# The first 128 queries' scores by products of 256 columns, the two halves added by VectorE

## The chip, the cores and the metric

The kernel runs on one core of a Trainium2 chip. The metric is the device time of one execution in microseconds; below 0.2% two times of this kernel count as the same. The operands and the output are float32.

## The reference, cut to what matters

One decoder layer over 512 tokens of width 1024: a gated linear recurrence (HGRN2) and a multi-head latent attention (MLA, 8 heads) side by side, then a gated merge, an output product and a norm. The change is in the scores of the attention:

```python
def attend_block(blk):                       # blocks of 128 queries
    qn = q_nope[block]; qp = q_pe[block]     # 128 and 64 numbers per head
    s = (einsum('bqhd,bkhd->bhqk', qn, k_nope)
         + einsum('bqhr,bkr->bhqk', qp, k_pe)) * scale
    s = where(q_pos[:, None] >= key_pos[None, :], s, -inf)
    p = softmax(s, axis=-1)
    return einsum('bqhk,bkhd->bqhd', p, v)
```

`k_pe` is one rotary key for all heads. For the first 128 queries only the first 128 keys count.

## The kernel before, in words

**Numbers.** TensorE multiplies float32 values as pairs: a high part (the value rounded to the `F32R` format) and a low part (the rest). `split` (L158) makes them: ScalarE casts the high part (L160), VectorE subtracts it to get the low part (L161). `mm3` (L88) is a product of two such pairs: high by high (L91), high by low (L92), low by high (L93), three matmuls into one PSUM bank. Each matmul loads its own stationary operand (a weight load, PEld in the profile) and streams a moving one, 512 columns in most of them.

**Scores.** `mla_scores` (L708) treats the 512 queries of a head in four blocks of 128. Block `i` needs `n = 128 (i + 1)` keys, so its matmuls have 128, 256, 384 and 512 columns. Each block has five: three of `mm3` on the parts of q and k without position, and two (L718) with the rotary query, whose high and low parts lie in the two halves of the partitions, against the rotary key's high part and low part (`kpe[0]`, `kpe[1]`). VectorE then adds the causal mask onto the last 128 columns in PSUM (L721), takes the row maximum (L722) and scales it (L723); ScalarE takes the exponential (L724); VectorE inverts its sum (L725); GpSimd multiplies by that (L726; VectorE in the last head). Then TensorE transposes the result (L742).

**Order.** Head 0's scores stand in a TensorE order written out by hand (`last_outputs`). Those of heads 1 to 7 are placed by a planner, which simulates every engine by costs of its own and issues what is ready first by program order; so TensorE's order between the scores and the neighbouring products (the gate of the head, the keys and queries of the next one, the output of the one before) is the planner's. All queues are served in order once laid out.

**Tiles.** A pool hands out tiles by tag; with one buffer for a tag, whatever first writes a new tile of that tag waits until all that used the old one has ended. `qn`, `kn` and `qp` were two tiles each, one for the high and one for the low part (tags `qn0`, `qn1` and so on), `kpe` too. The tags of `qn`, `kn` and `qp` in the pool `ma_pool` serve twice: for the heads, and long before (71 to 110 us) in `early_sums` (L801), which forms sums of blocks of the normed input while the recurrence runs. Its `keep` (L811) splits a sum and stores both parts to DRAM from SP's queue (L815). `keep` runs four times per call with the tags qn, kn, qp, qn, and `early_sums` is called twice.

**PSUM.** Three of the eight banks (`mm_ps`, `N_MM = 3`) hold projections, five (`ax_ps`) the rest.

Of the kernel before, what the change touches and what calls it, by code (L numbers as in the profile page):

```python
# [9 lines left out]
F32 = mybir.dt.float32  # L10
F32R = mybir.dt.float32r
# [3 lines left out]
ALU = mybir.AluOpType  # L15
# [3 lines left out]
P = 128  # L19
D = 1024  # L20
S = 512
# [17 lines left out]
def hybrid_layer(ctx: ExitStack, tc: tile.TileContext, a):  # L39
    nc = tc.nc  # L40
# [13 lines left out]
    def mm_tile():  # L54
        return mm.tile([P, 512], F32, tag="mm", name="mm_ps")

    def ax_tile():
        return ax.tile([P, 512], F32, tag="ax", name="ax_ps")
# [4 lines left out]
    class Pool:  # L63


        def __init__(self, name, side):
            self.cm = tc.tile_pool(name=name, bufs=1, side=side, reuse_waits="tile")
            self.p = self.cm.__enter__()
# [16 lines left out]
    cpool = Pool("cpool", "right")  # L85


    def mm3(ps, l, r, lsl, rsl, start, stop):  # L88

        (lh, ll), (rh, rl) = l, r  # L90
        nc.tensor.matmul(ps, lh[lsl], rh[rsl], start=start, stop=False)  # L91
        nc.tensor.matmul(ps, lh[lsl], rl[rsl], start=False, stop=False)  # L92
        nc.tensor.matmul(ps, ll[lsl], rh[rsl], start=False, stop=stop)  # L93
# [5 lines left out]
    def load_w(*pieces, to=None):  # L99

        raw = wraw.tile([P, WCH], F32, tag="raw", name="w_raw")
        hi, lo = to or [pool.tile([P, WCH], F32R, tag=tag, name=f"w_{tag}")[:] for pool, tag in ((whi, "hi"), (wlo, "lo"))]
        views, o = [], 0
        for src in pieces:
            n = int(np.prod(src.shape[1:]))
            if len(src.shape) == 4:
                _, k, h, c = src.shape
                dst = raw[:, o : o + n].rearrange("p (k h c) -> p k h c", k=k, h=h)
                for i in range(k):
                    nc.sync.dma_start(dst[:, i], src[:, i])  # L110
            else:
                last_dma[0] = nc.sync.dma_start(raw[:, o : o + n].rearrange("p (k c) -> p k c", k=src.shape[1]), src)
                if queued:
                    with tc.issue_after(last_dma[0].ins):
                        queued.pop(0)()
            views.append([t[:, o : o + n].rearrange("p (k c) -> p k c", k=src.shape[1]) for t in (hi, lo)])
            o += n
        last_hi[0] = nc.scalar.copy(hi[:, :o], raw[:, :o])  # L118
        last_lo[0] = nc.vector.tensor_tensor(lo[:, :o], raw[:, :o], hi[:, :o].bitcast(F32), op=ALU.subtract)  # L119
        return views[0] if len(views) == 1 else views  # L120
# [6 lines left out]
    def proj_ch(mat, c0, rhs, hook=None):  # L127

        ps = [mm_tile() for _ in range(2)]
        for kh, w in enumerate(load_cols(mat, c0)):  # L130
            for m in range(2):
                if hook and kh and m:
                    hook()
                for k in range(4):
                    kk = 4 * kh + k
                    mm3(ps[m][:], w, rhs, (slice(None), k, slice(m * P, m * P + P)),
                        (slice(None), kk), kk == 0, kk == KD - 1)
        return ps
# [19 lines left out]
    def split(hi, lo, src):  # L158

        nc.scalar.copy(hi, src)  # L160
        nc.vector.tensor_tensor(lo, src, hi.bitcast(F32), op=ALU.subtract)  # L161
# [5 lines left out]


    cT = [cpool.tile([P, 5, S], F32R, f"cT{i}") for i in range(2)]
    kpe = [cpool.tile([P, S], F32R, f"kpe{i}") for i in range(2)]  # L170
    cw = Pool("cwork", "right")
    ktab = cw.tile([P, NT, 2, NR], F32, "ktab")
    c_sb = cw.tile([P, NT, 704], F32, "c_sb")
# [182 lines left out]
    ps = ax_tile()  # L356
# [9 lines left out]
    mask_inf = const.tile([P, P], F32, name="mask_inf")  # L366
# [23 lines left out]
    for t in range(NT):  # L390
        ps = mm_tile()
        for k in range(KD):
            mm3(ps[:, 0:448], hT, c_second[k // 2], (slice(None), k, slice(t * P, t * P + P)), (slice(None), k % 2),
                k == 0, k == KD - 1)
        nc.scalar.copy(c_sb[:, t, 256:704], ps[:, 0:448])
# [18 lines left out]
    for j in range(5):  # L414
        ps = ax_tile()
# [5 lines left out]
    ps = ax_tile()  # L421
    for t in range(NT):
        nc.tensor.transpose(ps[:, t * P : t * P + P], kd[:, t].rearrange("p a r -> p (a r)"), ident[:])
    split(kpe[0][:], kpe[1][:], ps[:])
    cw.close()


# [1 line left out]
    ma_pool = Pool("mla_a", "right")  # L429
# [197 lines left out]
    def low(w, k0, nk):  # L627
        ps = mm_tile()
        for k in range(nk):
            mm3(ps[:], w, cT, (slice(None), k), (slice(None), k0 + k), k == 0, k == nk - 1)  # L630
        return ps
# [21 lines left out]

    def mla_rope_hi(qr, qx):

        qp, qh = [ma_pool.tile([P, S], F32R, f"qp{i}") for i in range(2)], ma_pool.tile([P, S], F32R, "qh")
        with tc.issue_after(last_act[0].ins):
            nc.scalar.copy(qh[:], qx[:])
            for i in range(2):
                own = slice(64 * i, 64 * i + 64)  # L660
                nc.scalar.copy(qp[i][own], qr[own])
        return qp, qh, qx
# [9 lines left out]
    def mla_rope(qr, qx):  # L672
        return mla_rope_lo(*mla_rope_hi(qr, qx))
# [12 lines left out]
    def mla_nope(h, pool):  # L686
        wq, wk = load_w(w_uq[:, :, h, 0:128], w_ukv[:, :, h, 0:128])
        res = []
        for w, k0, nk, nm in ((wq, 0, 3, "qn"), (wk, 3, 2, "kn")):
            ps = low(w, k0, nk)  # L690
            t = [pool.tile([P, S], F32R, f"{nm}{x}") for x in range(2)]
            split(t[0][:], t[1][:], ps[:])
            res.append(t)
        return res

    def mla_gate(h, hook=None):
# [11 lines left out]
    def mla_scores(h, pool, qn, kn, qp, final=False):  # L708

        pn = []  # L710
        for i in range(NT):
            n = (i + 1) * P
            bl = slice(i * P, n)
            sps = ax_tile()
            qh = qp[h % 2]
            mm3(sps[:, :n], qn, kn, (slice(None), bl), (slice(None), slice(0, n)), True, False)
            for x in range(2):
                nc.tensor.matmul(sps[:, :n], qh[:, bl], kpe[x][:, :n], start=False, stop=x == 1)  # L718
            sm = pool.tile([P, 4], F32, "sm", 4)
            p = pool.tile([P, n], F32, f"p{i}")  # L720
            nc.vector.tensor_tensor(sps[:, bl], sps[:, bl], mask_inf[:], op=ALU.add)  # L721
            nc.vector.tensor_reduce(sm[:, 0:1], sps[:, :n], axis=AX.X, op=ALU.max, negate=True)  # L722
            nc.vector.tensor_scalar(sm[:, 1:2], sm[:, 0:1], SCALE, None, op0=ALU.mult)  # L723
            last_act[0] = nc.scalar.activation(p[:, :n], sps[:, :n], AF.Exp, scale=SCALE, bias=sm[:, 1:2], accum_out=sm[:, 2:3])  # L724
            last_dve[0] = nc.vector.reciprocal(sm[:, 3:4], sm[:, 2:3])  # L725
            scaled_p = (nc.vector if final else nc.gpsimd).tensor_scalar(p[:, :n], p[:, :n], sm[:, 3:4], 0.5,  # L726
                                                                         op0=ALU.mult, op1=ALU.mult)
            if not final:
                last_pool[0] = scaled_p
            pn.append(p)  # L730
        return pn
# [28 lines left out]
    def minus(out, x, y):  # L760
        nc.vector.tensor_tensor(out, x, y, op=ALU.subtract)

    def minus_minus(out, x, y):

        nc.vector.scalar_tensor_tensor(out, x, -1.0, y, op0=ALU.mult, op1=ALU.subtract)
# [33 lines left out]
    h_dram = [[dram.tile([P, 4, 256], F32, name=f"h{n}{i}") for i in range(2)] for n in range(1, 5)]  # L799

    def early_sums(q):  # L801

        E = lambda tag: ma_pool.tile([P, 2, 256], F32, tag)[:]
        h11, h12, h21, h22 = zip(*[[b[:, q] for b in blocks(t)] for t in hT])

        def whole(tag, hl):
            out = E(tag)
            nc.vector.tensor_tensor(out, hl[0].bitcast(F32), hl[1].bitcast(F32), op=ALU.add)
            return out

        def keep(n, tag, src):  # L811
            hl = [ma_pool.tile([P, 2, 256], F32R, f"{tag}{i}") for i in range(2)]
            split(hl[0][:], hl[1][:], src)
            for i in range(2):
                nc.sync.dma_start(h_dram[n - 1][i][:, q], hl[i][:].bitcast(F32))  # L815

        e22, e21, e11, e12 = whole("qr", h22), whole("qs", h21), whole("qh", h11), whole("p3", h12)
        minus(e22, e22, e21)
        keep(1, "qn", e22)
        minus_minus(e22, e22, e11)  # L820
        keep(2, "kn", e22)
        minus(e21, e11, e21)
        keep(3, "qp", e21)
        minus_minus(e12, e12, e22)
        keep(4, "qn", e12)
# [115 lines left out]
    qp, nope, pn = early  # L941
    late = None
    turned_q = mla_turn(1)
    for h in range(H):
# [5 lines left out]
        if h % 2 and h + 1 < H:  # L950
            qp = mla_rope(*turned_q)
# [292 lines left out]
```

## Time and profile before

| | |
|---|---|
| median of 3 runs | 612.52 us (612.38 to 612.58) |
| the profiled execution | 612.32 us, of which 610.5 us lie between its first and its last instruction |
| TensorE (PE) busy | 600.0 us, 98% |
| VectorE (DVE) busy | 434.5 us, 71% |
| ScalarE (ACT) busy | 285.4 us, 47% |
| GpSimd (POOL) busy | 151.8 us, 25% |
| matmuls of the scores | start from 272.9 to 392.3 us |

Times in the rows are us from the first instruction. A row's duration of a matmul holds its way through the array, so durations of neighbours overlap; what a matmul costs TensorE is the distance to the next one's start. A few matmul records are missing.

### The profile page before, as it was taken

How to read it: one execution, taken by the hardware profiler on the slowest of the kernel's cores; microseconds unless marked ns; L12 is line 12 of the kernel's file. 1: busy time of each engine (PE TensorE's matmuls, PEld its weight loads, DVE VectorE, ACT ScalarE, POOL GpSimd, SP SyncE). 2: the span in 40 equal slices, each digit the busy share in tenths (PEclk: the TensorE clock that was granted, in tenths of full speed). 3: DMA queues.
4: the chain of work that ended last, by engine and by line, in shares of the span. 5: the costliest groups of instructions: out<-in, count | busy, mean ns of one | idle time of the engine just before them, and what ended most of it. 6: DMA issues, size and time to landing. Idle time of an engine off the chain costs nothing.

```text
span 610.5 us, 9790 instructions
## 1 busy us (share of the span) xinstructions
PE 600.0 (98%) x3686; PEld 526.6 (86%) x3686; DVE 434.5 (71%) x679; ACT 285.4 (47%) x531; POOL 151.8 (25%) x253
## 2 busy tenths in 40 slices
PE   8999999999999999999999999999999999999994
PEld 5998888888888888888888888899999999888884
DVE  7717988589874639958767766747757678567885
ACT  5555245323313242435646455438757853434352
POOL 4106322354360136414263620400000000000011
PEclk9999999999999999999999999999999999999998
DMA  7549479996979966673469574956665565695103
GB/s 266 165 138 337 160 216 377 295 233 145 251 161 269 235 177 143 140 156 96 59 177 157 143 149 120 246 214 213 191 189 179 186 196 169 198 365 176 42 27 139
DMA packets 74544, 114.38 MB, mean 187 GB/s; under 512 B 7512, under 2 KB 41726, under 8 KB 74496
## 3 DMA queue, kind: packets, MB, share of 16 engines
q1 hardware_dynamic: 65100, 89.69, 45.7%
q0 software_dynamic: 8336, 22.55, 20.2%
q10 hardware_dynamic: 1060, 1.51, 0.7%
q8 instruction: 29, 0.48, 0.3%
q14 instruction: 19, 0.16, 0.1%
HBM read 105.34 MB, written 39.85 MB: 238 GB/s over the span
## 4 chain that ended last, share of the span: by engine, by line
PE 89%; DVE 6%; ACT 2%; issue 1%; DMA 0%; POOL 0%; POOLq 0%; ACTq 0%; DVEq 0%
PE mm_ps L91 19%; PE mm_ps L92 19%; PE mm_ps L93 19%; PE ax_ps L883 16%; PE mm_ps L883 3%; PE ax_ps L718 2%; PE mm_ps L271 1%; PE ax_ps L742 1%; PE ax_ps L551 1%; DVE w_lo L119 1%; DVE ya L1115 1%; PE ax_ps L93 1%; PE ax_ps L92 1%; PE ax_ps L91 1%; PE ax_ps L553 1%
## 5 line engine op out<-in xcount | busy, mean ns | idle before, releaser
L119 DVE TENSOR_TENSOR w_lo<-w_raw,w_hi 128x1024 fp32r<-128x1024 f32 (+3 forms) x116 | 137.2, 1196 | 75.3 <-ACT w_hi L118 69.5
L118 ACT CAST w_hi<-w_raw 128x1024 fp32r<-128x1024 f32 (+3 forms) x116 | 114.9, 1006 | 133.8 <-PE mm_ps L92 64.7
L91 PE MATMUL mm_ps<-hT,w_hi 128*128 128x512 f32 x320 | 125.9, 394 | 0.0
L92 PE MATMUL mm_ps<-hT,w_hi 128*128 128x512 f32 x320 | 125.2, 391 | 0.0
L93 PE MATMUL mm_ps<-hT,w_lo 128*128 128x512 f32 x320 | 124.8, 391 | 0.0
L93 PEld LDWEIGHTS mm_ps<-hT,w_lo 128*128 128x128 f32 x320 | 60.1, 188 | 12.3
L91 PEld LDWEIGHTS mm_ps<-hT,w_hi 128*128 128x128 f32 x320 | 60.1, 188 | 12.1
L92 PEld LDWEIGHTS mm_ps<-hT,w_hi 128*128 128x128 f32 x320 | 60.1, 188 | 11.7
L883 PE MATMUL ax_ps<-s,w_hi 128*128 128x256 f32 x384 | 54.1, 283 | 0.0
L883 PEld LDWEIGHTS ax_ps<-s,w_hi 128*128 128x128 f32 x384 | 49.7, 192 | 0.1
L1132 POOL TENSOR_SCALAR ssum<-ssum 128x1 f32<-128x1 f32 x3 | 0.9, 312 | 188.5 <-ACT sq L1119 188.5
L93 PE MATMUL mm_ps<-w_hi,hT 128*128 128x512 f32 (+1 forms) x96 | 36.5, 382 | 0.0
L92 PE MATMUL mm_ps<-w_lo,hT 128*128 128x512 f32 (+1 forms) x96 | 36.5, 382 | 0.0
L91 PE MATMUL mm_ps<-w_hi,hT 128*128 128x512 f32 (+1 forms) x96 | 36.2, 386 | 0.0
L724 ACT ACTIVATE p<-ax_ps,sm 128x128 f32<-128x128 f32 (+3 forms) x32 | 16.9, 528 | 34.4 <-DVE sm L723 34.0
L726 POOL TENSOR_SCALAR p<-p,sm 128x128 f32<-128x128 f32 (+3 forms) x28 | 15.7, 562 | 66.1 <-DVE sm L723 40.2
L883 PE MATMUL ax_ps<-s,w_lo 128*128 128x256 f32 x192 | 31.3, 284 | 0.2 <-DVE w_lo L119 0.2
L883 PEld LDWEIGHTS ax_ps<-s,w_lo 128*128 128x128 f32 x192 | 26.6, 192 | 0.4 <-DVE w_lo L119 0.4
L461 DVE RECIPROCAL tf<-pr 128x512 f32<-128x512 f32 x8 | 26.8, 3348 | 0.1
L91 PE MATMUL mm_ps<-cT,w_hi 128*128 128x512 f32 x52 | 20.7, 398 | 0.0
L93 PEld LDWEIGHTS mm_ps<-w_hi,hT 128*128 128x128 f32 x96 | 18.0, 188 | 3.1
L91 PEld LDWEIGHTS mm_ps<-w_hi,hT 128*128 128x128 f32 x96 | 18.0, 188 | 2.9
(299 smaller groups left out, 1211.3 us busy)
## 6 DMA issues: line engine op xcount, KB each, us to landing
w_raw<-w_in SPq DMA_DIRECT2D x54, 512.0 KB, 6.4
g_t<-w_in SPq DMA_DIRECT2D x16, 512.0 KB, 8.8
w_raw<-g_t SPq DMA_DIRECT2D x16, 512.0 KB, 4.3
g_t<-w_in POOLq DMA_DIRECT2D x8, 512.0 KB, 9.8
pa_t<-w_proj_a SPq DMA_DIRECT2D x8, 512.0 KB, 12.7
g_t<-g_t POOLq DMA_DIRECT2D x8, 512.0 KB, 10.1
out_t<-w_out SPq DMA_DIRECT2D x8, 512.0 KB, 8.6
s<-h POOLq DMA_DIRECT2D x8, 512.0 KB, 11.3
```

The costliest lines, as they stand in the source:

```text
L91: nc.tensor.matmul(ps, lh[lsl], rh[rsl], start=start, stop=False)
L92: nc.tensor.matmul(ps, lh[lsl], rl[rsl], start=False, stop=False)
L93: nc.tensor.matmul(ps, ll[lsl], rh[rsl], start=False, stop=stop)
L118: last_hi[0] = nc.scalar.copy(hi[:, :o], raw[:, :o])
L119: last_lo[0] = nc.vector.tensor_tensor(lo[:, :o], raw[:, :o], hi[:, :o].bitcast(F32), op=ALU.subtract)
L271: nc.tensor.matmul(ps, hT[l][:, 4 * kh + k, t * P : t * P + P], c_hl[kh][r][:, k * 256 : k * 256 + 256], start=kh == 0 and kind == 0 and k ...
L461: nc.vector.reciprocal(rp[:], pr[:])
L551: nc.tensor.matmul(ops[:, sl], asb[:, sl], v_sb[i][:, (h % 4) * P : (h % 4) * P + P], start=True, stop=i == 0)
L718: nc.tensor.matmul(sps[:, :n], qh[:, bl], kpe[x][:, :n], start=False, stop=x == 1)
L724: last_act[0] = nc.scalar.activation(p[:, :n], sps[:, :n], AF.Exp, scale=SCALE, bias=sm[:, 1:2], accum_out=sm[:, 2:3])
L726: scaled_p = (nc.vector if final else nc.gpsimd).tensor_scalar(p[:, :n], p[:, :n], sm[:, 3:4], 0.5, op0=ALU.mult, op1=ALU.mult)
L883: nc.tensor.matmul(ps[:, o], w[k // 2][i][:, k % 2, cols], ap[j][:, k], start=not banks and c == 0 and n == 0, stop=n == 11, skip_group_ch ...
```

## The change

A class `Pair` makes one tile of 2 x 512 columns look like the list of two that it replaces; `kpe`, `qn`, `kn`, `qp` and the tiles of `keep` become such pairs, high and low part side by side. In block 0 of each head the matmul against the key's high part and the one against its low part become one of 256 columns whose moving operand is two runs of 128 (columns 0 to 127 of the high part, and of the low part). The bank then holds two halves of partial scores, and VectorE adds the second half and the mask into the tile `p0`, and that onto the first half.

```diff
-    kpe = [cpool.tile([P, S], F32R, f"kpe{i}") for i in range(2)]
+    kpe = Pair(cpool.tile([P, 2, S], F32R, "kpe")[:])
...
-        qp, qh = [ma_pool.tile([P, S], F32R, f"qp{i}") for i in range(2)], ma_pool.tile([P, S], F32R, "qh")
+        qp, qh = Pair(ma_pool.tile([P, 2, S], F32R, "qp")[:]), ma_pool.tile([P, S], F32R, "qh")
...
-            t = [pool.tile([P, S], F32R, f"{nm}{x}") for x in range(2)]
-            split(t[0][:], t[1][:], ps[:])
-            res.append(t)
+            res.append(Pair(pool.tile([P, 2, S], F32R, nm)[:]))
+            split(*res[-1], ps[:])
...
-            mm3(sps[:, :n], qn, kn, (slice(None), bl), (slice(None), slice(0, n)), True, False)
-            for x in range(2):
-                nc.tensor.matmul(sps[:, :n], qh[:, bl], kpe[x][:, :n], start=False, stop=x == 1)
+            if i == 0:
+                wide = sps[:, : 2 * P].rearrange("p (x k) -> p x k", x=2)
+                nc.tensor.matmul(wide, qn[0][:, bl], kn.both[:, :, bl], start=True, stop=False)
+                nc.tensor.matmul(sps[:, bl], qn[1][:, bl], kn[0][:, bl], start=False, stop=False)
+                nc.tensor.matmul(wide, qh[:, bl], kpe.both[:, :, bl], start=False, stop=True)
+            else:
+                mm3(sps[:, :n], qn, kn, (slice(None), bl), (slice(None), slice(0, n)), True, False)
+                for x in range(2):
+                    nc.tensor.matmul(sps[:, :n], qh[:, bl], kpe[x][:, :n], start=False, stop=x == 1)
...
-            nc.vector.tensor_tensor(sps[:, bl], sps[:, bl], mask_inf[:], op=ALU.add)
+            if i == 0:
+                nc.vector.tensor_tensor(p[:], sps[:, P : 2 * P], mask_inf[:], op=ALU.add)
+            nc.vector.tensor_tensor(sps[:, bl], sps[:, bl], mask_inf[:] if i else p[:], op=ALU.add)
...
-            hl = [ma_pool.tile([P, 2, 256], F32R, f"{tag}{i}") for i in range(2)]
-            split(hl[0][:], hl[1][:], src)
+            hl = Pair(ma_pool.tile([P, 2, 2, 256], F32R, tag)[:])
+            split(*hl, src)
```

## Rows read from the trace of the kernel before

**Rows 1.** The page: TensorE's share, then the chain that ended last by engine.
```profile
PE 600.0 (98%) x3686; PEld 526.6 (86%) x3686; DVE 434.5 (71%) x679; ACT 285.4 (47%) x531; POOL 151.8 (25%) x253
...
PE 89%; DVE 6%; ACT 2%; issue 1%; DMA 0%; POOL 0%; POOLq 0%; ACTq 0%; DVEq 0%
```

**Rows 2.** Waits from 200 to 420 us, TensorE's: us in total, times, longest.
```profile
engine line waited for: us in total, times, longest us
...
PEld ax_ps L883 <- DVE w_lo L119: 0.4, 1, 0.4
...
PE ax_ps L883 <- DVE w_lo L119: 0.2, 1, 0.2
```

**Rows 3.** Chain of waits in order of time, where attention ends: start, us, what.
```profile
411.60 0.13 PE mm_ps L92
...
411.75 1.71 ACT ma L1000 x4
```

**Rows 4.** Timeline of TensorE, head 0's blocks 0 and 1: start, us, engine, line, operation.
```profile
272.86 0.22 PE L91 MATMUL ax_ps<-kn,qn 128*128 128x128 f32 x1
272.92 0.28 PE L92 MATMUL ax_ps<-kn,qn 128*128 128x128 f32 x1
273.03 0.27 PE L93 MATMUL ax_ps<-kn,qn 128*128 128x128 f32 x1
273.15 0.38 PE L718 MATMUL ax_ps<-kpe,qp 128*128 128x128 f32 x2
273.37 0.34 PE L91 MATMUL ax_ps<-kn,qn 128*128 128x256 f32 x1
273.54 0.28 PE L92 MATMUL ax_ps<-kn,qn 128*128 128x256 f32 x1
273.66 0.28 PE L93 MATMUL ax_ps<-kn,qn 128*128 128x256 f32 x1
273.77 0.40 PE L718 MATMUL ax_ps<-kpe,qp 128*128 128x256 f32 x2
274.01 0.34 PE L91 MATMUL ax_ps<-kn,qn 128*128 128x384 f32 x1
...
275.11 0.40 PE L92 MATMUL ax_ps<-kn,qn 128*128 128x512 f32 x1
275.34 0.40 PE L93 MATMUL ax_ps<-kn,qn 128*128 128x512 f32 x1
```

**Rows 5.** Chain in order of time: runs of 128 columns (L742) and 256 (L883).
```profile
314.61 1.09 PE ax_ps L742 x10
...
401.91 2.88 PE mm_ps L883 x24
```

**Rows 6.** Timeline of VectorE, head 6: mask add, then the maximum that reads it.
```profile
375.04 0.30 DVE L721 TENSOR_TENSOR ax_ps<-ax_ps,mask_inf 128x128 f32<-128x128 f32 x1 [2.68 <-PE ax_ps L718]
375.44 0.29 DVE L722 TENSOR_REDUCE sm<-ax_ps 128x1 f32<-128x128 f32 x1
```

**Rows 7.** Busy time by engine over the attention, 272 to 411 us, four stretches summed.
```profile
sum 139.00, PE 139.00 PEld 121.97 DVE 96.20 ACT 71.29 POOL 48.82; mean PE 34.75 PEld 30.49 DVE 24.05 ACT 17.82 POOL 12.20
```

**Rows 8.** Timelines of GpSimd and TensorE, head 6: last scaling and first transposes.
```profile
381.52 0.70 POOL L726 TENSOR_SCALAR p<-p,sm 128x512 f32<-128x512 f32 x1 [1.70 <-DVE sm L725]
...
382.40 0.82 PE L742 MATMUL ax_ps<-ident,p 128*128 128x128 f32 x6
```

**Rows 9.** Timelines of SP, ScalarE, VectorE and TensorE around the second `early_sums`.
```profile
86.78 0.56 SPq L815 DMA_DIRECT2D h<-qn x1
...
91.94 0.61 ACT L160 CAST qn<-qr 128x512 fp32r<-128x512 f32 x1
92.46 0.59 ACT L488 ACTIVATE f<-mm_ps 128x512 f32<-128x512 f32 x1
...
93.81 0.68 DVE L491 SCALAR_TENSOR_TENSOR f<-f,mm_ps 128x512 f32<-128x512 f32 x1
94.58 0.69 DVE L161 TENSOR_TENSOR qp<-qs,qp 128x512 fp32r<-128x512 f32 x1
...
97.06 0.69 DVE L161 TENSOR_TENSOR qn<-qr,qn 128x512 fp32r<-128x512 f32 x1 [1.18 <-DMA h<-qn]
...
93.20 0.47 PE L92 MATMUL mm_ps<-hT,w_hi 128*128 128x512 f32 x1
```

More of the change, by code (lines that the diff above doesn't have):

```diff
@@ L85, in hybrid_layer, with __init__, __getitem__, __iter__ @@
     cpool = Pool("cpool", "right")
+    class Pair:
+        def __init__(self, both):
+            self.both = both
+        def __getitem__(self, i):
+            return self.both[:, i]
+        def __iter__(self):
+            return iter((self[0], self[1]))
     def mm3(ps, l, r, lsl, rsl, start, stop):
@@ L423, in hybrid_layer @@
         nc.tensor.transpose(ps[:, t * P : t * P + P], kd[:, t].rearrange("p a r -> p (a r)"), ident[:])
-    split(kpe[0][:], kpe[1][:], ps[:])
+    split(*kpe, ps[:])
     cw.close()
@@ L811, in keep @@
         def keep(n, tag, src):
-            hl = [ma_pool.tile([P, 2, 256], F32R, f"{tag}{i}") for i in range(2)]
-            split(hl[0][:], hl[1][:], src)
+            hl = Pair(ma_pool.tile([P, 2, 2, 256], F32R, tag)[:])
+            split(*hl, src)
             for i in range(2):
-                nc.sync.dma_start(h_dram[n - 1][i][:, q], hl[i][:].bitcast(F32))
+                nc.sync.dma_start(h_dram[n - 1][i][:, q], hl[i].bitcast(F32))
         e22, e21, e11, e12 = whole("qr", h22), whole("qs", h21), whole("qh", h11), whole("p3", h12)
```

## The prediction

> **What bounds the kernel now.** I read the page first: TensorE is busy for 98% of the span, and 89% of the chain that ended last is TensorE's own [rows 1]. A share is an average, so the next view is that of the waits, cut to the stretch with the attention. There the reader is to see how little TensorE's instructions wait: between 200 and 420 us, behind VectorE, they wait once, 0.2 us for a matmul and 0.4 for its weight load, for the low part of a weight, and never for the softmax of the scores [rows 2]. The busy times of 272 to 411 us say the same: TensorE 139.0 of 139.0 us, VectorE 96.2 of them, ScalarE 71.3, GpSimd 48.8 [rows 7]. So in the stretch of the scores a slot taken from TensorE is time gained, if what replaces it stays hidden. The chain leaves TensorE once near by, at 411.75 us, for a ScalarE activation; but what ended the matmul just before it at 411.73 (411.60 + 0.13) released that activation [rows 3]. That stretch begins where TensorE brings it, and moves with it.
>
> **What a matmul of 128 columns costs.** A row's duration contains its way through the array, so the price is read from starts. Head 0's first block: five matmuls of 128 columns start at 272.86 and the next block's first starts at 273.37, 0.51 us. The next five, of 256 columns, take 273.37 to 274.01, 0.64 us. The ten together take 1.15 us, 0.115 each [rows 4]. Elsewhere ten in a row of 128 columns take 1.09 us, 0.109 each, and 24 of 256 columns 2.88 us, 0.120 each [rows 5]. Twice the columns cost 0 to 10% more, whereas 512 columns cost 0.23 (275.11 to 275.34) [rows 4]. So below 256 columns a matmul costs a slot of about 0.11 us, whatever it streams. The second start of the first block, 0.06 us after the first, is no counterexample: it is given back at the block's end, where 256 columns take 0.17 (273.37 to 273.54) instead of 0.115.
>
> *A rule that speaks against the change.* The Trainium skill (TensorE: Matmul & The Clock Gate, section Back-to-back issue gap) gives a matmul by itself N / 2.4 + 2.5 ns. By it the five cost 5 x 55.8 = 279 ns and the three of 256, 128 and 256 columns 109 + 56 + 109 = 274 ns, as an estimate from that page: nothing would be gained, since both stream 640 columns. The measured 0.51 us for the five disagrees, so the sum is not made by it; it stays as a rival below.
>
> **The parts of the change.**
> 1. TensorE, block 0 of each of 8 heads: five slots become three (256, 128, 256 columns). Two slots go: 2 x 0.109 = 0.22 to 2 x 0.115 = 0.23 us a head. If the wide slots cost the 0.120 of the 256-column run, 5 x 0.109 - (0.120 + 0.109 + 0.120) = 0.196. So 1.57 to 1.84 us over 8 heads. I take 0.22 a head, 1.75 us, nearest to the pair of blocks that stands in this very place.
> 2. The wide moving operand is two runs of 128 columns with 384 between them. No matmul of the trace reads such a one. Bounds: from below the 0.115 of a plain 256; from above the 0.23 of 512 columns, as if each column took two steps. That would be 16 x 0.115 = 1.84 us dearer and eat the gain. I take the lower end: the same number of columns is read, in two long runs.
> 3. VectorE gets one more addition of 128 columns a head. Its price is the row of the mask add: 0.30 us long, and what reads its result starts 0.40 us after it [rows 6]. So 8 x 0.30 = 2.4 us of VectorE, and each head's block 0 is 0.40 us later towards its exponential, of which some 0.2 comes back because TensorE finishes the block earlier. VectorE is 42.8 us idle in the stretch [rows 7], which covers the load. Behind the added instruction wait the other blocks' additions and maxima, ScalarE's exponentials, GpSimd's scalings and in the end the transposes. The tightest place that I found is head 6: GpSimd's last scaling ends at 382.22, and the first transposes start at 382.40 [rows 8]; the one that needs it is the fourth, 3 x 0.109 = 0.33 us on. 0.51 us of room against 0.40 of delay: nothing is lost. If the cover failed in every head it would cost 8 x 0.40 = 3.2 us; if in one or two, 0.2 to 0.8. I take 0, as no wait of TensorE there hangs on this chain now.
> 4. The temporary goes into `p0`, which is free by then, and PSUM's five banks are used as before: 0.
> 5. Larger tiles. `kpe`, and `qn`, `kn`, `qp` of the heads: the readers of both parts end in the same scores, and a new pair is written a head or two later, so nothing waits longer: 0. In `early_sums` it is different. Before, the copy of a new high part waited for the store of the old high part; now it waits for both stores. Only where the second store is late does that count: the tag `qn` is used again soonest. The first call's last low part is stored from 86.78 us, and VectorE waited for its landing until 97.06 [rows 9]. ScalarE's copy of the next high part ran at 91.94 without it; now it has to wait until 97.06 too. Bounds: 0 if the planner puts it behind what TensorE needs, 3 us if not (last rival). I take 0.
>
> Sum: -1.75 us. Against the profiled execution's own 612.32 us that is 610.57; its time is 0.20 below the median of the runs, so for the median 612.52 - 1.75 = 610.77. I forecast **610.8 us**, 610.3 to 611.3 for this case by itself (-2.2 with a stall or two of the size in [rows 2] lost by a luckier order, -1.2 with as much gained).
>
> **Rivals.**
> - *Columns, not slots.* If streaming sets the price, by either of two ways: each column costs the same and 640 stay 640, or the split operand takes 0.23 us. Both end at 612.5 (-1.84 + 1.84 for the second). Against the first speaks that 256 columns cost as much as 128 in [rows 4] and [rows 5]; against the second nothing in the trace. The Trainium skill (PSUM — Partial Sum Buffer, Specifications (TRN2)) says that a non-contiguous access slows matmuls significantly; the output here stays contiguous in PSUM, only the operand in SBUF is split, and no run here shows either.
> - *VectorE's chain becomes what the transposes wait for*, in the heads where the planner has them close behind (head 6). Two to four heads with 0.2 to 0.4 us: +0.4 to +1.6, so 611.2 to 612.4. For it: the room of 0.51 us in head 6, and that the planner orders by its own estimates, so that other orders may come out. Against it: no wait for this chain in [rows 2].
> - *Slower: ScalarE held up by a store.* Suppose that ScalarE's queue keeps its order at 91.94 us. The copy waits until 97.06 and takes 0.61; only then does the activation of 92.46 run, 97.67 to 98.26, and VectorE's reader of the same projection bank, 0.68 long, ends at 98.94. With three projection banks, the second half of the next projection needs this bank 12 matmuls after its first. One of its first matmuls starts at 93.20 [rows 9], so it is due at 93.2 + 12 x 0.23 = 96.0. TensorE stands for 98.9 - 96.0 = 2.9 us, and the sum is 612.52 - 1.75 + 2.9 = 613.7, 0.2% slower. It decides from the point where ScalarE's copy stands ahead of that activation in the queue. For it: VectorE's subtraction for the same tile did wait 1.18 us, so the planner thought the landing earlier than it was. Against it: VectorE's queue has the subtraction for `qp` (94.58) ahead of that for `qn`, against program order, so the planner knew that the store lands after 94 us, and would put ScalarE's copy behind the activation as well; then ScalarE waits about 1 us where nothing urgent follows.
>
> **How the numbers follow.** Forecast as reasoned: 0.60. Columns: 0.12 (0.04 for the even price per column, which the trace contradicts, 0.08 for the split operand). VectorE's chain: 0.15. Store: 0.13. What a measurement can tell from no change is 0.2%, 1.2 us: below 611.3 is faster, above 613.7 slower. The forecast's case is faster, 0.60; columns and VectorE's chain are mostly the same, 0.27; the store is slower, 0.13. The range for 8 in 10 reaches from 610.2 over the two middle rivals to 613.0 and leaves out the last one and a little below.
>
> **What would show it.** Right: 16 matmuls fewer in the scores; the first block of a head 0.28 to 0.30 us from its first start to the next block's, where it was 0.51; no new wait of TensorE between 272 and 411 us; 8 additions more on VectorE of 0.3 us each. Wrong: a wide matmul followed after 0.2 us or more (operand); a wait in front of a transpose (VectorE's chain); ScalarE idle for some microseconds near 92 us with a DMA as releaser and TensorE waiting behind a projection bank (store). The prediction fails if the end of the attention, now 411.7 us, moves by much other than 1.75 us, or if what follows it does not move along.

## The result and the profile after

| | before | after |
|---|---|---|
| median | 612.47 us (13 runs) | 611.08 us (13 runs) |
| profiled execution | 612.32 us, span 610.5 | 611.30 us, span 609.4 |

The ratio is 0.9976 with a 95% interval of 0.9969 to 0.9983: 0.24% or 1.39 us faster, at the interval's ends 0.17% and 0.31%. The forecast was 610.8 us, 1.75 us faster. One of the 13 runs took 2766.76 us; it is left out of the ratio, and nothing here says what it was.

The page of the changed kernel, in the rows that answer to [rows 1]:

```profile
PE 598.4 (98%) x3670; PEld 524.5 (86%) x3670; DVE 438.9 (72%) x687; ACT 285.4 (47%) x531; POOL 149.1 (24%) x253
...
PE 89%; DVE 6%; ACT 2%; issue 1%; DMA 0%; POOL 0%; POOLq 0%; ACTq 0%; DVEq 0%
```

TensorE has 16 matmuls fewer (3686 to 3670), VectorE 8 instructions more (679 to 687), and the chain is TensorE's as before. The timeline of TensorE in head 0, blocks 0 and 1, answers to [rows 4]:

```profile
273.24 0.28 PE L728 MATMUL ax_ps<-kn,qn 128*128 128x256 f32 x1
273.35 0.22 PE L729 MATMUL ax_ps<-kn,qn 128*128 128x128 f32 x1
273.41 0.34 PE L730 MATMUL ax_ps<-kpe,qp 128*128 128x256 f32 x1
273.58 0.28 PE L102 MATMUL ax_ps<-kn,qn 128*128 128x256 f32 x1
273.70 0.28 PE L103 MATMUL ax_ps<-kn,qn 128*128 128x256 f32 x1
273.81 0.28 PE L104 MATMUL ax_ps<-kn,qn 128*128 128x256 f32 x1
273.93 0.40 PE L734 MATMUL ax_ps<-kpe,qp 128*128 128x256 f32 x2
274.17 0.34 PE L102 MATMUL ax_ps<-kn,qn 128*128 128x384 f32 x1
```

The two blocks take 0.93 us (273.24 to 274.17) where they took 1.15: 0.22 us less. The first wide matmul is followed after 0.11 us, no later than one with a plain operand of 256 columns. The second is followed after 0.17, but the narrow one in front of it after only 0.06, so these two together take 0.23, two slots.

To see where the gain stays, I compare three starts of TensorE in each profiled execution (e1 to e8 are the experiments further down): the first matmul of the scores, the first transpose of head 7's softmax, and the first matmul of the product with `w_proj_b`, which stands behind the merge gates and the product with `w_proj_a`. Differences of such starts leave out what the beginning of an execution varies by. "Scores" is the time from the first to the second start, "gates" from the second to the third; the scores' stretch holds 725 matmuls before and 709 after, the gates' 934 in both.

| kernel | first score | head 7's transposes | `w_proj_b` | scores, against before | gates, against before |
|---|---|---|---|---|---|
| before | 272.86 | 404.63 | 517.58 | | |
| after | 273.24 | 403.26 | 516.49 | -1.75 | +0.28 |
| after, once more (e8) | 272.94 | 402.97 | 516.18 | -1.74 | +0.26 |
| tiles only (e1) | 273.14 | 404.91 | 517.87 | 0.00 | +0.01 |
| tiles in turn (e2) | 273.07 | 403.10 | 516.31 | -1.74 | +0.26 |
| narrow (e3) | 273.03 | 402.92 | 515.34 | -1.88 | -0.53 |
| one more add (e4) | 272.84 | 402.91 | 516.14 | -1.70 | +0.28 |
| cast first (e5) | 273.35 | 403.38 | 515.80 | -1.74 | -0.53 |
| before, cast first (e6) | 273.26 | 405.03 | 517.84 | 0.00 | -0.14 |
| both (e7) | 273.33 | 403.35 | 515.77 | -1.75 | -0.53 |

For example, (403.26 - 273.24) - (404.63 - 272.86) = -1.75. The scores give the whole of what was forecast. The next stretch gives 0.28 back, and the beginning varies by more than that from one execution to the next.

**What is given back behind the attention.** The waits of TensorE between 200 and 420 us answer to [rows 2]. There are now two kinds, one of them behind ScalarE:

```profile
engine line waited for: us in total, times, longest us
...
PEld ax_ps L901 <- ACT w_hi L129: 0.5, 1, 0.5
...
PEld ax_ps L901 <- DVE w_lo L130: 0.3, 1, 0.3
PE ax_ps L901 <- ACT w_hi L129: 0.2, 1, 0.2
```

The timeline of ScalarE shows why:

```profile
405.25 1.06 ACT L129 CAST w_hi<-w_raw 128x1024 fp32r<-128x1024 f32 x1
410.36 1.71 ACT L1018 ACTIVATE ma<-c,hb_gate 128x256 f32<-128x256 f32 x4 [4.05 <-PE mm_ps L103]
411.97 1.13 ACT L171 CAST q<-ya 128x512 fp32r<-128x512 f32 x2
413.00 1.05 ACT L129 CAST w_hi<-w_raw 128x1024 fp32r<-128x1024 f32 x1
413.96 0.58 ACT L917 ACTIVATE part<-ax_ps 128x512 f32<-128x512 f32 x1
414.44 1.03 ACT L129 CAST w_hi<-w_raw 128x1024 fp32r<-128x1024 f32 x1
```

ScalarE stands idle for 4.05 us in front of four activations that wait for the last head's output, while the cast behind them, for the next weights of the gate, has only its data to wait for. That cast comes at 413.00. In the kernel before, both casts followed one another from 414.40; now a copy of a bank (L917) stands between them, so the second half of the weights is later against TensorE.

The kernel before lost time there too. The waiting matmul after, and the one before, in TensorE's timelines:

```profile
415.53 0.98 PE L901 MATMUL ax_ps<-s,w_hi 128*128 128x256 f32 x6 [0.25 <-ACT w_hi L129]
...
417.89 0.50 PE L883 MATMUL ax_ps<-s,w_lo 128*128 128x256 f32 x2 [0.23 <-DVE w_lo L119]
```

Set against e5, where no matmul of this stretch waits, the changed kernel loses 0.51 us around 415.53 and 0.30 around 416.79, the kernel before about 0.5 around 417.89. The 0.28 in the table is the difference of the two.

**What is given back in the recurrence.** In this one execution the matmuls before the scores lost 0.27 us more than in the kernel before: between the same two starts lie 152.99 us (104.89 to 257.88), before 152.72 (104.79 to 257.51). Timelines of ScalarE, VectorE and TensorE of the changed kernel:

```profile
111.26 0.62 ACT L171 CAST qn<-p 128x512 fp32r<-128x512 f32 x1 [4.91 <-DMA h<-qn]
...
111.91 0.69 DVE L172 TENSOR_TENSOR qn<-p,qn 128x512 fp32r<-128x512 f32 x1 [3.92 <-ACT qn L171]
112.53 2.40 DVE L553 COPY_PREDICATED asb<-mask_le,ax_ps 64x512 f32<-64x512 uint8 x4
...
113.47 0.39 PE L103 MATMUL mm_ps<-hT,w_hi 128*128 128x512 f32 x1
113.85 0.68 PE L562 MATMUL ax_ps<-v,asb 128*128 128x128 f32 x4
```

The second call's last high part waits for a store of the tile that it reuses; VectorE's subtraction behind it, and behind that the copies of the recurrence's masked scores, which TensorE needs next. The matmul at 113.85 starts 0.38 us after its predecessor, where a matmul of 512 columns is followed after 0.23. The view of waits puts the 0.4 us in front of its weight load down to an earlier matmul (L104); that the copies released it is read from the times. The first two of the four are about 0.72 and 0.45 us long and end at 113.7; in e1 they start at 111.54, and there the matmul does not wait.

### The profile page after: what moved, and what is told of

It reads as the page before. It is cut to its first block, busy times and chain, and to the rows that moved or that the text cites. A ratio compares the mean times of both kernels' runs of the same rounds, so it can differ in the third digit from the quotient of the medians.

```text
span 609.4 us, 9767 instructions
## 1 busy us (share of the span) xinstructions
PE 598.4 (98%) x3670; PEld 524.5 (86%) x3670; DVE 438.9 (72%) x687; ACT 285.4 (47%) x531; POOL 149.1 (24%) x253
## 4 chain that ended last, share of the span: by engine, by line
PE 89%; DVE 6%; ACT 2%; issue 1%; DMA 0%; POOL 0%; POOLq 0%; ACTq 0%; DVEq 0%
PE mm_ps L102 19%; PE mm_ps L103 19%; PE mm_ps L104 19%; PE ax_ps L901 16%; PE mm_ps L901 3%; PE mm_ps L282 1%; PE ax_ps L760 1%; PE ax_ps L734 1%; PE ax_ps L562 1%; DVE w_lo L130 1%; DVE ya L1133 1%; PE ax_ps L564 1%; PE ax_ps L524 1%; PE ax_ps L104 1%; PE ax_ps L103 1%
## 5 line engine op out<-in xcount | busy, mean ns | idle before, releaser
L130 DVE TENSOR_TENSOR w_lo<-w_raw,w_hi 128x1024 fp32r<-128x1024 f32 (+3 forms) x116 | 138.8, 1207 | 67.9 <-ACT w_hi L129 66.0
L104 PE MATMUL mm_ps<-hT,w_lo 128*128 128x512 f32 x320 | 125.1, 392 | 0.0
L104 PEld LDWEIGHTS mm_ps<-hT,w_lo 128*128 128x128 f32 x320 | 60.1, 188 | 12.3
L104 PE MATMUL mm_ps<-w_hi,hT 128*128 128x512 f32 (+1 forms) x96 | 36.5, 382 | 0.0
L742 ACT ACTIVATE p<-ax_ps,sm 128x128 f32<-128x128 f32 (+3 forms) x32 | 16.7, 525 | 35.5 <-DVE sm L741 33.0
L104 PEld LDWEIGHTS mm_ps<-w_hi,hT 128*128 128x128 f32 x96 | 18.0, 188 | 3.0
```

## The experiments

Each ran beside the kernel before, e1 to e4 on one chip and e5 to e8 on another.

**e1: the large tiles alone.** Block 0 and its mask as before.

```diff
-            if i == 0:
-                wide = sps[:, : 2 * P].rearrange("p (x k) -> p x k", x=2)
...
-            else:
-                mm3(sps[:, :n], qn, kn, (slice(None), bl), (slice(None), slice(0, n)), True, False)
+            mm3(sps[:, :n], qn, kn, (slice(None), bl), (slice(None), slice(0, n)), True, False)
```

> The large tiles alone: qn, kn, qp, kpe and the tiles of early_sums are pairs, but block 0 has its five matmuls of 128 columns and one mask addition as before. Theory (two matmul slots a head are worth 1.74 us, and about 0.3 us is given back where the larger tiles of early_sums make a copy wait for a store): 612.7 to 612.9, that is 0.2 to 0.4 above before, with ScalarE waiting some microseconds for a store near 110 us and a gap of about 0.25 us in front of the recurrence's outputs near 114 us. Rival (the part given back comes from the wide matmuls or from VectorE's added addition): 612.4 to 612.6, no such gap.

612.54 us, ratio 1.0002 (0.9993 to 1.0011). ScalarE waited 3.77 us for the store, until 110.28, but TensorE had no gap near 114 us. The theory's 0.2 to 0.4 did not come: the tiles are free within what can be measured. The loss behind the late store in the changed kernel's profile is a matter of that one execution.

**e2: tiles in turn.**

```diff
+        tags = ("qn", "kn", "qp", "qn") if q == kh[0] else ("kn", "qp", "qn", "kn")
...
-        keep(1, "qn", e22)
+        keep(1, tags[0], e22)
```

> The change, but early_sums takes its tiles in turn (qn, kn, qp, qn in the first call, kn, qp, qn, kn in the second), so that a tile comes back after three keeps and not after one. Theory (reuse of qn while its second store is under way holds ScalarE, then VectorE, then TensorE): 610.8, about 0.26 below the changed kernel, no gap near 114 us. Rival (the wait for the store costs the end nothing): 611.1, as the changed kernel.

611.43 us, ratio 0.9984 (0.9975 to 0.9993). No gap near 114 us, as expected, yet not faster than the changed kernel but 0.2 to 0.4 above it. Its profiled execution started the scores 0.21 us late (273.07), most of which it had lost by 55 us, before any of these tiles is used. The intervals of the two overlap. So a gain of 0.26 is not shown, and the theory of e1 and e2 falls as an account of the median.

**e3: narrow matmuls in the same three slots.** Products with the key's low part are left out in block 0.

```diff
-                nc.tensor.matmul(wide, qn[0][:, bl], kn.both[:, :, bl], start=True, stop=False)
+                nc.tensor.matmul(sps[:, bl], qn[0][:, bl], kn[0][:, bl], start=True, stop=False)
...
-                nc.tensor.matmul(wide, qh[:, bl], kpe.both[:, :, bl], start=False, stop=True)
+                nc.tensor.matmul(sps[:, bl], qh[:, bl], kpe[0][:, bl], start=False, stop=True)
...
-                nc.vector.tensor_tensor(p[:], sps[:, P : 2 * P], mask_inf[:], op=ALU.add)
+                nc.vector.tensor_tensor(p[:], sps[:, bl], mask_inf[:], op=ALU.add)
```

> The change with both wide matmuls cut to the 128 columns of the key's high part; the products with its low part in block 0 are left out, and the added addition reads the first half. Same number of matmuls, 16 x 128 columns fewer. Theory (a slot has one price up to 256 columns): 610.9 to 611.1, at most 0.1 below the changed kernel (0.120 against 0.115 a slot). Rival (columns set the price, 0.053 us for 128 of them): 16 x 0.053 = 0.85 below, 610.2.

609.99 us, ratio 0.9960 (0.9947 to 0.9972), 1.1 us below the changed kernel. By the total alone the rival (0.85) would have won. The table says otherwise: over the scores only 0.14 us more were saved (-1.88 against -1.74), and 0.8 came behind the attention, where the planner happened to put the cast ahead of the four activations. The timeline of TensorE in head 0 of this kernel:

```profile
273.03 0.22 PE L727 MATMUL ax_ps<-kn,qn 128*128 128x128 f32 x1
273.09 0.28 PE L728 MATMUL ax_ps<-kn,qn 128*128 128x128 f32 x1
273.20 0.27 PE L729 MATMUL ax_ps<-kpe,qp 128*128 128x128 f32 x1
273.31 0.33 PE L102 MATMUL ax_ps<-kn,qn 128*128 128x256 f32 x1
...
273.96 0.34 PE L102 MATMUL ax_ps<-kn,qn 128*128 128x384 f32 x1
```

273.03 to 273.96 is 0.93 us, the same as with the wide ones. At 128 and at 256 columns a slot has one price, to within 0.14 / 16 = 0.009 us. (TensorE's order in the scores came out otherwise in this kernel, so not all of the 0.14 need be the columns'.) It also raised the question that e5 to e7 answer.

**e4: one more addition on VectorE.**

```diff
+                nc.vector.tensor_tensor(p[:], p[:], mask_inf[:], op=ALU.add)
```

> The change with one more addition of the mask into the temporary in block 0 of each head, which depends on the one before it (8 x 0.30 us of VectorE, 0.4 us later towards the exponential). Theory (VectorE's addition is hidden under TensorE): 611.1, as the changed kernel, within 0.15. Rival (the added addition costs what is missing of the 1.75 us): another 0.3 on top, 611.4.

611.02 us, ratio 0.9980 (0.9971 to 0.9989): nothing added to the total. Over the scores -1.70, 0.04 us less saved than with one addition. TensorE's order within that stretch came out otherwise too, so what the 0.04 is stays open. VectorE's additions are hidden.

**e5: the cast first.** The loads of the first block sum and of half of the second move ahead of the activations in the text, and an ordering edge puts the activations behind the cast. In ScalarE's order this one cast moves and nothing else; VectorE's subtraction for the low part of the same weight moves with it.

```diff
...
-    for b, ps in later:
-        closed("c11", 0, 0, 1.0, gate_out(0, lambda j: ma[:, j]))(b, ps)
+    w1 = gate_w[0].sum(1)
+    w2 = load_w(gate_w[0].t[1][:, kh[0]])
+    with tc.issue_after(last_hi[0].ins):
+        for b, ps in later:
+            closed("c11", 0, 0, 1.0, gate_out(0, lambda j: ma[:, j]))(b, ps)
...
```

> The change, and one cast of a weight's high part (first half of the second block sum of the first merge gate) placed ahead of the four activations that wait for the last head's output at 410.4 us; nothing else in ScalarE's order differs. Theory (the changed kernel gives back 0.3 us between 410 and 417 us because this cast stands behind those activations and a bank copy stands between the next two casts): the gaps of 0.52 and 0.32 us in front of the matmuls at 415.5 and 416.8 go, 0.8 us less than the changed kernel, 610.2. Rival (the gaps are due to the data of the weights landing late): no change, 611.0.

610.54 us, ratio 0.9967 (0.9954 to 0.9979), 0.65 below the changed kernel on the same chip (e8); the table has the expected 0.8 (+0.28 to -0.53). About 0.5 of it is what the kernel before lost as well. The timeline of ScalarE:

```profile
409.54 1.05 ACT L129 CAST w_hi<-w_raw 128x1024 fp32r<-128x1024 f32 x1 [3.11 <-DMA w_raw<-g_t]
410.49 1.71 ACT L1018 ACTIVATE ma<-c,hb_gate 128x256 f32<-128x256 f32 x4
412.11 1.13 ACT L171 CAST q<-ya 128x512 fp32r<-128x512 f32 x2
413.13 0.58 ACT L917 ACTIVATE part<-ax_ps 128x512 f32<-128x512 f32 x1
413.63 1.03 ACT L129 CAST w_hi<-w_raw 128x1024 fp32r<-128x1024 f32 x1
```

The cast runs as its data lands, at 409.54 instead of 413.00, the activations are not later for it, and TensorE runs through (a row of its timeline there):

```profile
415.00 1.12 PE L901 MATMUL ax_ps<-s,w_hi 128*128 128x256 f32 x8
```

Between 410 and 418 us no matmul waits any more. This execution lost some 0.3 us elsewhere, at 81.95 us, in front of a matmul of the recurrence's gate. Its waits from 81 to 82.4 us show for what, the low part of a weight:

```profile
PEld mm_ps L104 <- DVE w_lo L130: 0.3, 1, 0.3
```

e1, e6 and e7 have the same wait (0.2 to 0.5 us), the changed kernel does not.

**e6: the cast first in the kernel before.** The same edit.

> The kernel before with the same cast placed ahead. Theory: its one gap there, 0.50 us at 417.9, goes: 611.9 to 612.0. The distance to the changed kernel with the same cast first is then 1.74 us, the whole of the two slots a head. Rival (no gap of this kernel hangs on that order): 612.4.

612.61 us, ratio 1.0001 (0.9992 to 1.0010): the expected 0.5 did not come; the table has 0.14, and TensorE still waits there once, 0.2 us for the low part of a weight. The timeline of ScalarE:

```profile
407.89 1.07 ACT L118 CAST w_hi<-w_raw 128x1024 fp32r<-128x1024 f32 x1
412.19 1.05 ACT L118 CAST w_hi<-w_raw 128x1024 fp32r<-128x1024 f32 x1 [3.23 <-PE mm_ps L92]
413.14 1.70 ACT L1000 ACTIVATE ma<-c,hb_gate 128x256 f32<-128x256 f32 x4
```

Here the cast holds up the activations by 0.95 us, since it can start only at 412.19. Its load was issued at 408.54, when the cast and subtraction of an earlier weight had freed its buffer, and landed at 412.11; in e5 the same load was issued at 405.50 and landed at 409.46. The changed kernel casts the weights before that one earlier (401.07, before 405.80), so its loads run earlier and the move pays there.

**e7: cast first and tiles in turn.**

> The change with the cast first and with the tiles of early_sums taken in turn. Theory: no gap near 114 us and none near 416 us; 610.2 less 0.03 to 0.28, so 609.9 to 610.2. Rival (the tiles in turn cost something, as the 611.4 of that kernel alone against 611.1 of the changed one may say): 610.5 or more.

610.41 us, ratio 0.9964 (0.9951 to 0.9976): the best version with the whole output, 0.13 below e5, which is within the scatter. e8, the changed kernel again:

> The changed kernel once more, beside the others on one chip: 611.1, 0.2% below before.

611.19 us, ratio 0.9978 (0.9969 to 0.9987).

## Why the prediction was right, and where not

**TensorE, two slots a head: right to 0.01 us.** Forecast 1.75, measured 1.74 to 1.75 in the five executions whose scores are those of the change (after, e2, e5, e7, e8), and 1.70 in e4, with one more addition. The measured price of a slot carried it. By the count of columns, the rival, the scores would have given nothing; e3 took 16 x 128 columns out of the same slots and gained 0.14 us, not 0.85. The formula of the Trainium skill that stood beside that rival (TensorE: Matmul & The Clock Gate, Back-to-back issue gap) is given there for a matmul by itself; the page says that it counts too little where columns are few, since it leaves out the weight load. It does not price these matmuls, each of which has a weight load of its own: 56 ns by it for 128 columns, 0.11 us here.

One sign came out otherwise than I had named it: a head's first block takes 0.34 us (273.24 to 273.58), not 0.28 to 0.30. The short start of 0.06 us now stands inside the block and is given back at its end; the next block is the shorter one, 0.59 us (273.58 to 274.17) where it was 0.64. Only the two together show the 0.22.

That "below 256 columns a matmul costs a slot of about 0.11 us, whatever it streams" was too wide. The price of 0.11 us is shown for 128 and 256 columns with a stationary operand of 128x128. The kernel before has narrower matmuls, with 64 columns in both operands, in TensorE's timeline:

```profile
104.79 1.15 PE L527 MATMUL ax_ps<-qi,ki 128*64 128x64 f32 x32
```

These 32 take 1.15 us together, 0.036 each.

**The split operand: right.** The lower end held: 0.11 us to the next start behind the first wide matmul, and two slots, 0.23, for the narrow and the second wide one together. This case shows no slowing by an operand in two runs of 128 columns.

**VectorE's addition: right, for a reason that I had partly wrong.** The timeline of VectorE in head 6 answers to [rows 6]:

```profile
374.26 0.29 DVE L738 TENSOR_TENSOR p<-ax_ps,mask_inf 128x128 f32<-128x128 f32 x1 [2.90 <-PE ax_ps L730]
374.59 0.30 DVE L739 TENSOR_TENSOR ax_ps<-ax_ps,p 128x128 f32<-128x128 f32 x1
...
375.00 0.62 DVE L740 TENSOR_REDUCE sm<-ax_ps 128x1 f32<-128x128 f32 x2
```

From the first addition to the maximum it is 0.74 us, where it was 0.40: 0.34 more, against the 0.40 taken. Between 272 and 411 us the view of waits has no wait of TensorE in the changed kernel. But the room in head 6 was not 0.51 us. I had read the fourth of the six transposes as the one that needs the last scaling. In e4 GpSimd's scaling and TensorE's six transposes stand so (timelines):

```profile
380.72 0.69 POOL L745 TENSOR_SCALAR p<-p,sm 128x512 f32<-128x512 f32 x1 [1.91 <-DVE sm L744]
...
380.81 0.82 PE L761 MATMUL ax_ps<-ident,p 128*128 128x128 f32 x6
```

The fourth starts at 380.81 + 3 x 0.11 = 381.14, before the scaling's end at 381.41, and TensorE does not wait. So the six are those of the first three blocks, and the four that need the last block come later. The cover was wider than I thought.

**The stretch behind the attention: wrong.** The step that failed is that it "begins where TensorE brings it, and moves with it". It does begin there, but what follows is an order on ScalarE that the planner made anew, and 0.26 to 0.28 us of the gain went into it in four of the executions (after, e2, e4, e8). e5 takes one cast out of that order and gets 0.81 back, which shows that this order holds TensorE up. That the copy between the two casts makes the 0.28 against the kernel before is read from the timelines; no run moved the copy alone. My range had room for such a loss, "a stall or two" either way, but I put it at nothing in the sum, and as a rival I named other orders only for VectorE's chain.

**The store that holds ScalarE: the mechanism came, twice, at a smaller price.** Timeline of ScalarE in the changed kernel, which answers to [rows 9]:

```profile
92.02 0.59 ACT L499 ACTIVATE f<-mm_ps 128x512 f32<-128x512 f32 x1
...
97.83 0.62 ACT L171 CAST qn<-qr 128x512 fp32r<-128x512 f32 x1 [1.41 <-DMA h<-qn]
```

At 97.83 us ScalarE waited 1.41 us, behind the activation, as I had put it against the rival, and TensorE lost nothing. The second place I did not see: 4.91 us at 111.26, one reuse of the tag later. It cost 0.27 us in one execution and at most 0.04 in five others (e1, e3, e4, e5, e8) where the store landed between 109.0 and 110.6 us, which is why e1's median does not show it.

So 612.47 - 1.74 + 0.28 = 611.01, against the measured 611.08. What is left, 0.07, is below what these runs can tell. The profiled execution took 1.02 us less than its counterpart: it also lost 0.27 us in the recurrence and 0.10 before that (104.89 against 104.79), and -1.74 + 0.28 + 0.27 + 0.10 is -1.09.

## What to carry to other kernels

Read a matmul's price from start to start for the shape and weights at hand, and count slots where two widths cost the same: the fewer, wider matmuls are then worth the difference in slots, and a cheap addition on an engine with idle time pays for it. Where a planner orders the queues, a saving on the bounding engine is kept only where the queues that feed it are not reordered to its cost; look at the first place behind the edit where a feeding engine is idle in front of a waiting instruction, and ask what stands behind it. A total that agrees with a theory proves little at this size: e3's did for the wrong one, and only the time stage by stage told.

## What the runs showed that I had not expected

The first 55 us vary by 0.27 us between executions: the transposes of the first projections start at 54.64 in e4 and at 54.91 in e2, the same matmuls in both. The landing of one and the same store of 256 KB, the one that holds up the copy near 110 us, varied from 109.0 to 111.3 us. Both are as large as what was to be told here.
